# Two experts' weights by expert with conditional transfers, and a first mixer in another order

## The chip, the cores and the metric

The kernel runs on one NeuronCore of a Trainium2 chip. Its engines work side by side, each on its own queue: PE (TensorE, matmuls), DVE (VectorE), ACT (ScalarE), POOL (GpSimd) and SP (SyncE, which here issues the weight transfers). The metric is the device time of one execution in microseconds (us); lower is better.

## The reference, cut to what matters

256 tokens of width 1024 pass two blocks in float32. Each block is a mixer followed by a mixture of experts (MoE); 16 meta tokens stand ahead of the tokens in the first block.

```python
# block 1: mixer (latent attention + gated convolution), then experts
z = hp @ w_in                                   # q (256), kv (128), k_pe (32), three conv parts of 512
u = gate_c * x_in
conv = gate_b * sum(conv_w[k] * u_pad[:, k:k + plen] for k in range(3))
merged = concat([rms_norm(attn), rms_norm(conv)])
h = h + rms_norm(merged @ w_out)
# experts of a block: 4 groups of 8, best group, in it the best two experts
hid = silu(t @ w_gate[e]) * (t @ w_up[e]) * combine      # hidden 256 in block 1, 512 in block 2
routed = sum over e of hid @ w_down[e]
# end: final norm of the second block's output
```

Of 32 experts a token uses two, so an expert of the second block gets 16 tokens in the mean. On the reference's inputs the counts of the second block are 11 22 10 14 23 11 12 19 9 9 9 13 16 23 14 17 34 44 13 26 25 19 35 42 6 1 8 3 10 0 8 6: expert 29 has none.

## The kernel before, in words

Time is split into five stages: first mixer, first MoE, second mixer, second MoE, final norm. All weights are streamed from HBM in chunks of 1 MB ([128, 2048] float32) into 26 slots of SBUF. `plan()` gives the order of all chunks. `ahead()` and `load()` issue a chunk on SP's queue as soon as a slot is free and `fits()` finds that the tiles which the code takes later still have room. So SP's queue holds the transfers in plan order, and each may have to wait for the engine that last used its slot, and for the eighth transfer before it (eight can be under way).

The second MoE works in 16 pairs of experts, 64 places for each expert's tokens. For a pair: tokens are gathered by matmuls with one-hot matrices, `gate_up` (matmuls at L1501, 64 of them over 8 chunks, each of 128 rows of both experts' gate and up weights), silu and product (L1506, L1507), transposes (L1519), `down` (L1574, 32 matmuls over 4 chunks, each with both experts' weights), the products in two halves in a slot `ys`, and `scatter` (L1589), which adds them to the tokens' sums. `ys` is taken and freed for each pair. A chunk is freed as soon as its eight matmuls are done. The plan brings gate/up of a pair and then down of the pair before; at the end stand gate/up 14, down 13, down 14, gate/up 15 and down 15, the last in four quarters (L1544) by columns, each followed by its scatter (L1689), the squares of the final norm (L1182) and the product with its gain (L1184). A second path for experts with more than 64 tokens hangs on a branch and is not taken.

The first mixer, in order of code: PE transposes x (L432) and the meta tokens (L434); ScalarE and VectorE split them in two float32r halves `xh`, `xl`. A float32 product is made of three matmuls, high by high, high by low and low by high (`mm3`, L319 to L321). Weights are split in the same way: `prepare()` writes the high half on ScalarE (L294) and the low half on VectorE or GpSimd (L295). The first projection (q, kv and k_pe of all tokens) gives `cn` after normalisation (L524 to L541) and rotation (L549 to L552). Then convolution part 0 (`conv(0)`, 4 column groups of 24 matmuls, evacuated by L569 into `u`), the block of q and kv (transposes of `cn` at L576 to L593, L606 to L625), part 1 (`conv(1)`), q's transposes (L649), part 2 (`conv(2)`), the scores of 8 heads for two blocks of 128 queries (L679, L681; maximum L682, exponential L685), and the output projection `w_out` in four input quarters i: i = 0 and 1 behind the scores, then the transposes of the probabilities (`turn_p`, L727), then i = 2 and 3 around the attention of either block (`attend`, L742, L747). PSUM has 8 banks, taken in turn.

The steps above are written out by hand in the code; no planner moves compute instructions, only the transfers.

## Time and profile before

| | |
|---|---|
| median of 3 runs | 936.5 us (935.39 to 937.39) |
| profiled execution | 936.15 us, of it the span from first to last instruction 934.4 us |
| mean granted TensorE clock | 0.956 of full |
| PE busy | 845.6 us (91%) |
| VectorE, ScalarE, GpSimd busy | 389.6, 227.0, 118.8 us |
| transferred | 340.88 MB, 365 GB/s in the mean |
| second MoE | about 490 to 926 us |

The slices of the page are 23.4 us long each. A row of the timeline gives start and length in us, engine, line, operation, result and operands by the program's names, and, in brackets, how long the engine stood before and what released it. Matmuls are pipelined, so lengths of neighbouring rows overlap.

### The profile page before, as it was taken

What the parts mean: (1) busy time and instruction counts of PE and PEld (TensorE: products, weight loads), DVE (VectorE), ACT (ScalarE), POOL (GpSimd) and SP (SyncE); (2) the same over time, 40 slices, a digit from 0 to 9 for tenths busy, and PEclk for the clock granted to TensorE, in tenths of its full rate; (3) what the DMA queues carried; (4) which work ended last, traced back from release to release, by engine and by line L of the source; (5) the groups of instructions that cost most, each with busy time, mean ns of one, the idle gap of its engine ahead of it and who ended that gap; (6) DMA issues with size and microseconds to landing.
All of it is one profiled execution on the core that took longest, in us unless ns stands there. A gap on an engine that the chain in (4) does not pass through costs nothing. (4 is left out here: it accounts for less than half of the span.)

```text
span 934.4 us, 12196 instructions
## 1 busy us (share of the span) xinstructions
PE 845.6 (91%) x4789; PEld 469.0 (50%) x4789; DVE 389.6 (42%) x789; ACT 227.0 (24%) x473; POOL 118.8 (13%) x83
## 2 busy tenths in 40 slices
PE   7999999997967858997989999999999998799995
PEld 4788775553431316996874443434343432334332
DVE  4867672443322368576451224232333331133313
ACT  5346522211110135372312102111111110011113
POOL 3322520000000047634300000000000000000002
PEclk9999999998977897997999999999999999899998
DMA  9925498999999999553799999999999999999994
GB/s 363 415 95 221 160 385 354 420 419 418 420 420 420 421 421 421 219 178 138 271 364 368 421 415 391 421 421 422 420 422 420 421 422 421 416 422 421 421 420 169
DMA packets 48631, 340.88 MB, mean 365 GB/s; under 512 B 5536, under 2 KB 6176, under 8 KB 8112
## 3 DMA queue, kind: packets, MB, share of 16 engines
q1 hardware_dynamic: 47408, 338.55, 88.7%
q10 hardware_dynamic: 1152, 1.41, 0.5%
q8 instruction: 42, 0.69, 0.3%
q14 instruction: 29, 0.24, 0.1%
HBM read 338.88 MB, written 1.05 MB: 364 GB/s over the span
## 5 line engine op out<-in xcount | busy, mean ns | idle before, releaser
L1501 PE MATMUL bank<-chunk,xe 128*64 128x512 f32 (+1 forms) x1536 | 293.6, 618 | 27.8 <-DMA chunk<-in_gu_dram 15.0
L1501 PEld LDWEIGHTS bank<-chunk,xe 128*64 128x64 f32 (+1 forms) x1536 | 88.0, 130 | 218.2 <-issue 197.6
L1574 PE MATMUL bank<-chunk,hids 128*64 128x512 f32 (+1 forms) x736 | 143.3, 618 | 19.9 <-DMA chunk<-in_dn_dram 19.4
L1574 PEld LDWEIGHTS bank<-chunk,hids 128*64 128x64 f32 (+1 forms) x736 | 40.8, 128 | 117.4 <-issue 75.5
L295 POOL TENSOR_TENSOR w<-chunk,w 128x1024 fp32r<-128x1024 f32 x28 | 69.7, 2497 | 78.2 <-ACT w L294 65.4
L1578 DVE SCALAR_TENSOR_TENSOR ys<-bank,wc,ys 128x512 fp32r<-128x512 f32 x46 | 34.5, 750 | 98.1 <-ACT ys L1577 98.1
L1507 DVE TENSOR_TENSOR hids<-bank,hids 128x512 f32<-128x512 f32 x12 | 8.3, 692 | 158.0 <-PE bank L1501 158.0
L1577 ACT ACTIVATE ys<-bank,wc 128x512 fp32r<-128x512 f32 x46 | 31.6, 687 | 143.8 <-PE bank L1574 135.3
L1184 POOL TENSOR_TENSOR out<-acc,rows 128x256 f32<-128x256 f32 x6 | 4.3, 730 | 439.2 <-DVE acc L1692 439.1
L294 ACT ACTIVATE w<-chunk 128x1024 fp32r<-128x1024 f32 x52 | 52.4, 1053 | 22.0 <-DVE w L295 11.5
L1596 DVE TENSOR_TENSOR acc<-acc,bank 128x512 f32<-128x512 f32 x84 | 52.1, 680 | 13.3 <-PE bank L1589 13.3
L1512 DVE SCALAR_TENSOR_TENSOR hids<-bank,misc,hids 128x256 f32<-128x256 f32 (+1 forms) x12 | 6.9, 572 | 113.9 <-ACT hids L1511 70.7
L1506 ACT ACTIVATE hids<-bank 128x512 f32<-128x512 f32 x12 | 7.2, 597 | 181.6 <-PE bank L1501 181.6
L1347 PEld LDWEIGHTS bank<-GS,h 128*128 128x128 f32 x384 | 45.5, 197 | 10.7 <-issue 5.1
L1589 PE MATMUL bank<-ys,GS 128*128 128x512 f32 x184 | 49.5, 408 | 1.3 <-ACT ys L1577 1.3
L1347 PE MATMUL bank<-GS,h 128*128 128x128 f32 x384 | 47.8, 284 | 1.6 <-DVE GS L1355 1.6
L1511 ACT ACTIVATE hids<-bank,misc 128x256 f32<-128x256 f32 (+1 forms) x12 | 6.5, 546 | 136.0 <-PE bank L1501 136.0
L295 DVE TENSOR_TENSOR w<-chunk,w 128x1024 fp32r<-128x1024 f32 x24 | 35.7, 1494 | 8.8 <-ACT w L294 8.7
L948 PE MATMUL bank<-w,xT 128*128 128x512 f32 x144 | 37.8, 422 | 0.6 <-DVE xT L902 0.6
L1589 PEld LDWEIGHTS bank<-ys,GS 128*128 128x128 f32 x184 | 32.5, 188 | 10.9 <-ACT ys L1577 2.2
L948 PEld LDWEIGHTS bank<-w,xT 128*128 128x128 f32 x144 | 29.0, 205 | 7.8 <-DVE xT L902 1.7
L860 POOL TENSOR_TENSOR xn<-h,rows 128x1024 f32<-128x1024 f32 x2 | 4.7, 2388 | 188.3 <-DVE misc L1557 188.3
(401 smaller groups left out, 1187.1 us busy)
## 6 DMA issues: line engine op xcount, KB each, us to landing
chunk<-in_gu_dram SPq DMA_DIRECT2D x192, 1024.0 KB, 19.8
chunk<-in_dn_dram SPq DMA_DIRECT2D x95, 1024.0 KB, 19.8
chunk<-in_wi_dram SPq DMA_DIRECT2D x12, 1024.0 KB, 19.5
chunk<-in_wo_dram SPq DMA_DIRECT2D x8, 1024.0 KB, 15.9
chunk<-in_wc_dram SPq DMA_DIRECT2D x6, 1024.0 KB, 13.6
chunk<-in_sgu_dram SPq DMA_DIRECT2D x2, 1024.0 KB, 9.5
chunk<-in_wa_dram SPq DMA_DIRECT2D x2, 832.0 KB, 6.9
h<-in_x_dram SPq DMA_DIRECT2D x2, 512.0 KB, 5.4
```

The source lines that it names most:

```text
L294: self.nc.scalar.activation(w[:, 0], raw, AF.Copy)
L295: (eng or (self.nc.vector, self.nc.gpsimd)[e]).tensor_tensor(w[:, 1], raw, w[:, 0].bitcast(F32), op=OP.subtract)
L948: PE.matmul(p[t], xT[x][:, 2 * i + k, t * 128:t * 128 + 128], w[:, s, k * 512:k * 512 + 512], start=i + x + s + k == 0, stop=i + x == 4 an ...
L1347: b.nc.tensor.matmul(self.pb[k // 4][:, k % 4 * 128:k % 4 * 128 + 128], b.h[:, t, k * 128:k * 128 + 128], G[:, t].bitcast(F32), start=t == ...
L1501: PE.matmul(g[i][e * C:e * C + C], xe[:, k, e * C:e * C + C], c[:, e, i * 512:i * 512 + 512], start=k == 0, stop=k == 7)
L1506: A.activation(hid, g[0], AF.Silu)
L1507: V.tensor_tensor(hid, g[1], hid, op=OP.mult)
L1574: PE.matmul(y[e * C:e * C + C], hT[:, o:o + C], c[:, f, e], start=q + f == 0, stop=fpc * q + f == FC - 1)
L1577: A.activation(ys[:, 0, i], y, AF.Copy, scale=wc)
L1578: V.scalar_tensor_tensor(ys[:, 1, i], y, wc, ys[:, 0, i].bitcast(F32), op0=OP.mult, op1=OP.subtract)
L1589: PE.matmul(ps[t], S[:, t * 128:t * 128 + 128], ys[:, i, e], start=i == 0, stop=i == 1)
L1596: V.tensor_tensor(o, b.h[:, t, sl] if new else o, p, op=OP.add)
```

## The change

Second MoE: a chunk of gate/up now holds 256 rows of one expert, and a chunk of down one expert's half of the columns; chunks 0, 2, .. are of the first expert, 1, 3, .. of the second. `gate_up` and `down` take two chunks at once and free both behind the sixteen matmuls, whose order is as before. Down of pair 15 keeps its form. A chunk that goes into a slot whose last tile was a second expert's chunk reuses that tile, and its transfer is made conditional on the expert's count being above zero (`some()`); the counts are copied to SBUF by VectorE behind the routing and read by SP, one load for each expert. `ys` is kept from the first to the last pair.

First mixer: x and the meta tokens come transposed from the host, so the transposes on PE are gone; x itself is loaded later, for the residual. Constants come in one transfer, the first weights in half transfers. 60 matmuls on a constant tile (`warm`) stand ahead. The sums for the norm of x stand ahead of the angles on VectorE. `conv(1)` follows `conv(0)`, q's transposes stand inside `conv(2)`, and four PSUM banks are held from the scores on for the output projection, whose products for i = 0 and 1 stand between the scores of the second block. i = 2 follows, and i = 3 stands between the transposes of the probabilities.

End: the last quarter's product with the gain moves into the final scaling.

```diff
@@ -96,8 +97,12 @@
...
-        gu = np.concatenate([wg, wu], 2).reshape(32 // x, x, 8, 128, 2 * fw).transpose(0, 2, 3, 1, 4)
-        dn = wd.reshape(32 // x, x, fw // (128 * fc), fc, 128, 2, 512).transpose(0, 5, 2, 4, 3, 1, 6)
+        if n == 2:
+            gu = np.concatenate([wg, wu], 2).reshape(16, 2, 4, 2, 128, 1024).transpose(0, 2, 1, 4, 3, 5)
+            dn = wd.reshape(16, 2, 4, 128, 2, 512).transpose(0, 4, 1, 3, 2, 5)
+        else:
+            gu = np.concatenate([wg, wu], 2).reshape(32 // x, x, 8, 128, 2 * fw).transpose(0, 2, 3, 1, 4)
+            dn = wd.reshape(32 // x, x, fw // (128 * fc), fc, 128, 2, 512).transpose(0, 5, 2, 4, 3, 1, 6)
...
@@ -164,7 +171,7 @@
...
-    yield from (("wa", 0), ("wa", 1), ("wc", 0), ("wc", 1), ("wuq",), ("wukv",), *[("wc", j) for j in range(2, 6)])
+    yield from (("wa", 0), ("wa", 1), *[("wc", j) for j in range(4)], ("wuq",), ("wukv",), ("wc", 4), ("wc", 5))
     yield from (("wo", 2), ("wo", 3), ("wo", 0), ("wo", 1), ("pmg",), ("sgu", 0), ("sgu", 1))
...
@@ -224,7 +233,11 @@
...
             self.note("free")
             if self.trace:
-                self.empty.append(self.held.pop(id(t))[0])
+                i = self.held.pop(id(t))[0]
+                self.empty.append(i)
+                if any(t is x for x in self.ended):
+                    self.same[i] = t
+                    self.ended = [x for x in self.ended if x is not t]
         self.ahead()
...
@@ -249,16 +262,35 @@
     def load(self):
         key = self.loads[self.loaded]
         self.loaded += 1
-        t = self.ready[key] = self.take([128, CH], "chunk", F32)
+        kept = key[0] in ("gu2", "dn2") and self.trace and self.same.get(self.empty[0])
+        if kept:
+            t = self.ready[key] = kept
+            self.held[id(t)] = (self.empty.popleft(), t)
+        else:
+            t = self.ready[key] = self.take([128, CH], "chunk", F32)
         o = 0
+        some = self.some(key) if kept else {}
         for ap in self.source(key):
-            self.nc.sync.dma_start(t[:, o:o + ap.shape[-1]], ap)
+            self.nc.sync.dma_start(t[:, o:o + ap.shape[-1]], ap, **some)
             o += ap.shape[-1]
...
+    def some(self, key):
+
+
+        if not self.counts or key[0] not in ("gu2", "dn2") or key[:2] == ("dn2", 15):
+            return {}
+        e = 2 * key[1] + key[2] % 2
+        if e not in self.loads_of:
+            self.loads_of[e] = self.nc.values_load(self.counts[0:1, e:e + 1], engines=[mybir.EngineType.SP],
+                                                   min_val=0, max_val=T)
+        return {"cond": self.loads_of[e] > 0}
 
...
+        self.warm(60)
+
+    def warm(self, n):
+
+        p = self.bank()
+        for _ in range(n):
+            self.nc.tensor.matmul(p[:, 0:128], self.onesb, self.onesb, start=True, stop=True)
...
+        xt = self.slot([128, 8, T], "xt")
+        nc.scalar.dma_start(cT[:, 128:256], self.a["mt"])
+        raw = {}
+        for j in range(2):
+            nc.sync.dma_start(xt[:, 4 * j:4 * j + 4].rearrange("p k t -> p (k t)"), self.a["xt"][j])
+            raw[j] = self.chunk("wa", j)
...
-        ps = [bank() for _ in range(8)]
-        for t in range(2):
-            for k in range(8):
-                PE.transpose(ps[k][:, NM + t * 128:NM + t * 128 + 128], h[:, t, k * 128:k * 128 + 128], id_)
-                if t == 0:
-                    PE.transpose(ps[k][:, 0:NM], meta[:, k * 128:k * 128 + 128], id_[:NM, :NM])
...
+        def conv(i, done, then=(), between=()):
             for m in range(4):
+                if m in then:
...
-        conv(0, lambda m, p: V.tensor_tensor(u[:, m], p, rxx, op=OP.mult))
+        conv(0, lambda m, p: V.tensor_tensor(u[:, m], p, rxx, op=OP.mult),
+             between={0: spread_rx})
...
+        conv(1, gated)
...
-        self.phase(0, 2)
-        conv(1, gated)
...
-        self.free(*xp)
+        conv(2, conv_done, {2: turn_q})
...
+        pc = {(t, e): bank() for t in range(2) for e in range(2)}
+        w = [self.part(0) for _ in range(2)]
+        rows = [(t, e, i) for i in range(2) for t in range(2) for e in range(2)]
...
+                if t:
+                    r = rows[h0]
+                    w_out(pc, mc, *r, w[r[2]])
...
-                (self.nc.vector if q == 3 else self.nc.gpsimd).tensor_tensor(
-                    made["out"][:, t, sl], moe.acc[:, t, sl], made["rows"][:, sl], op=OP.mult)
-
-        self.link = made, ss, r
+                if q < 3:
+                    self.nc.gpsimd.tensor_tensor(made["out"][:, t, sl], moe.acc[:, t, sl], made["rows"][:, sl],
+                                                 op=OP.mult)
...
+            A.activation(o[:, t, 0:512], o[:, t, 0:512], AF.Copy, scale=r[:, t:t + 1])
+            V.scalar_tensor_tensor(o[:, t, 768:D], moe.acc[:, t, 768:D], r[:, t:t + 1], made["rows"][:, 768:D],
+                                   op0=OP.mult, op1=OP.mult)
+            V.tensor_scalar(o[:, t, 512:768], o[:, t, 512:768], r[:, t:t + 1], None, op0=OP.mult)
...
+        if self.n == 2:
+            counts = self.part(32).bitcast(I32)
+            V.tensor_copy(counts, self.pr[:, 64:96])
+            if b.trace:
+                b.counts = counts
...
+            for k in range(0, 8 if n == 2 else 0, 2):
+                cs = [load(f"gu{n}", pair, k + e) for e in range(2)]
+                for kk in range(2):
+                    for i in range(2):
+                        for e in range(2):
+                            PE.matmul(g[i][e * C:e * C + C], xe[:, k + kk, e * C:e * C + C],
+                                      cs[e][:, kk * 1024 + i * 512:kk * 1024 + i * 512 + 512],
+                                      start=k + kk == 0, stop=k + kk == 7)
+                done(*cs)
...
-            ys = b.slot([128, 2, 2, 512], "ys", F32R)
+            if n == 1 or self.ys is None:
+                self.ys = b.slot([128, 2, 2, 512], "ys", F32R)
+            ys = self.ys
...
+                if n == 2:
+                    cs = [load(f"dn{n}", pair, 2 * i + e) for e in range(2)]
+                    for f in range(4):
+                        for e in range(2):
+                            PE.matmul(y[e * C:e * C + C], hT[:, f * 128 + e * C:f * 128 + e * C + C],
+                                      cs[e][:, f * 512:f * 512 + 512], start=f == 0, stop=f == 3)
+                    done(*cs)
...
-                if e:
+                if e and n == 1:
                     b.free(ys)
```

VectorE around convolution part 0 before (u is part 0's result, w a weight's low half, cT and kT belong to the q/kv block):

```order
L551 TENSOR_TENSOR gen_87<-gen_87 128x3x16
L552 TENSOR_TENSOR gen_87<-gen_87 128x3x16
L569 TENSOR_TENSOR u<-bank,gen_87 128x258
L295 TENSOR_TENSOR w<-chunk,w 128x1024
L569 TENSOR_TENSOR u<-bank,gen_87 128x258 x2
L295 TENSOR_TENSOR w<-chunk,w 128x1024
L569 TENSOR_TENSOR u<-bank,gen_87 128x258
L581 TENSOR_SCALAR cT<-bank,small 128x128
L588 TENSOR_SCALAR cT<-bank,small 128x256 x2
```

And now, in the same place (vy is the gated convolution):

```order
L600 TENSOR_TENSOR gen_143<-gen_143 128x3x16
L601 TENSOR_TENSOR gen_143<-gen_143 128x3x16
L622 TENSOR_TENSOR u<-bank,gen_143 128x258
L330 TENSOR_TENSOR w<-chunk,w 128x1024
L622 TENSOR_TENSOR u<-bank,gen_143 128x258 x2
L330 TENSOR_TENSOR w<-chunk,w 128x1024
L622 TENSOR_TENSOR u<-bank,gen_143 128x258
L631 TENSOR_TENSOR u<-bank,u 128x258
L634 SCALAR_TENSOR_TENSOR vy<-u,const_72,vy 128x256 x2
L330 TENSOR_TENSOR w<-chunk,w 128x1024
```

The rotation, the evacuation of part 0 and the two low halves keep their order; the first of these low halves (first w row) is that of part 1's first column group, and what follows is part 1's evacuation in place of the q/kv block's.

PE at the last scores of the second query block and the output projection before (kT by qT are scores, gen1 the mask, mc the convolution's output):

```order
L679 MATMUL bank_880<-kT_459,qT_656 128x272
L681 LDWEIGHTS gen1_87
L681 MATMUL bank_880<-gen1_87 128x128
L679 MATMUL bank_885<-kT_459,qT_656 128x272
L681 LDWEIGHTS gen1_87
L681 MATMUL bank_885<-gen1_87 128x128
L319 MATMUL bank_903<-w_716,mc_681 128x512
L320 MATMUL bank_903<-w_716,mc_681 128x512
L321 MATMUL bank_903<-w_716,mc_681 128x512
```

And now, at the fourth and fifth head:

```order
L744 MATMUL bank_906<-kT_622,qT_680 128x272
L746 LDWEIGHTS gen1_143
L746 MATMUL bank_906<-gen1_143 128x128
L354 MATMUL bank_849<-w_716,mc_681 128x512
L355 MATMUL bank_849<-w_716,mc_681 128x512
L356 MATMUL bank_849<-w_716,mc_681 128x512
L744 MATMUL bank_914<-kT_623,qT_680 128x272
L746 LDWEIGHTS gen1_143
L746 MATMUL bank_914<-gen1_143 128x128
L354 MATMUL bank_846<-w_772,mc_681 128x512
```

Each head's scores are now followed by three matmuls of the projection.

SP at the first conditional transfers, now (misc holds the counts; an ISA row is a register operation):

```order
L274 DMA chunk_4650<-in_gu2_dram 128x2048
L284 TENSOR_LOAD misc_4519
L284 ISA x2
L274 ISA
L274 DMA chunk_3733<-in_gu2_dram 128x2048
```

Before, these were the plain DMA rows alone, one behind the other; now a register operation stands ahead of each, and a load ahead of an expert's first.

## Rows read from the trace of the kernel before

**Rows 1.** The page's slices: rate of the transfers

```profile
GB/s 363 415 95 221 160 385 354 420 419 418 420 420 420 421 421 421 219 178 138 271 364 368 421 415 391 421 421 422 420 422 420 421 422 421 416 422 421 421 420 169
```

**Rows 2.** The chain that ended last: start us, us, what

```profile
830.80 19.82 DMA chunk<-in_dn_dram
...
890.44 19.82 DMA chunk<-in_gu_dram
```

**Rows 3.** Waits and timeline of PE, 815 to 913 us

```profile
PE bank L1574 <- DMA chunk<-in_dn_dram: 3.9, 9, 0.6
PE bank L1501 <- DMA chunk<-in_gu_dram: 1.9, 4, 0.6
829.15 13.95 PE L1501 MATMUL bank<-chunk,xe 128*64 128x512 f32 x64
843.30 1.94 PE L1574 MATMUL bank<-chunk,hids 128*64 128x512 f32 x8 [0.20 <-DMA chunk<-in_dn_dram]
...
850.66 1.94 PE L1574 MATMUL bank<-chunk,hids 128*64 128x512 f32 x8 [0.55 <-DMA chunk<-in_dn_dram]
```

**Rows 4.** Windows: length, busy PE, PEld, DVE, ACT, POOL, PEclk, DMA share, GB/s

```profile
490.00:495.00 5.00, 5.00 (x24) 1.54 (x22) 2.05 (x12) 3.45 (x8) 0.00 (x0) 0.96 0.49 170
535.00:545.00 10.00, 10.00 (x47) 3.87 (x47) 3.58 (x8) 0.53 (x2) 0.00 (x0) 1.00 0.99 398
560.00:575.00 15.00, 15.00 (x80) 6.95 (x80) 7.22 (x12) 3.71 (x7) 0.00 (x0) 1.00 0.96 371
600.00:780.00 180.00, 177.97 (x868) 72.50 (x866) 52.99 (x99) 22.50 (x40) 0.00 (x0) 1.00 1.01 421
```

**Rows 5.** Waits of SP's queue, 490 to 600 us: total, times, longest

```profile
SPq L255 <- PE bank L1501: 69.9, 34, 12.5
```

**Rows 6.** SP's register operation at L1654, ns min/median/max

```profile
L1654 SPq FUSED_REGOPS  x2: 159/170/181, 231.8 to 806.7; - x2
```

**Rows 7.** Timeline of PE in the first mixer

```profile
5.95 0.48 PE L432 MATMUL bank<-const,h 128*128 128x128 f32 x1 [5.95 <-DMA const<-in_c_dram]
...
10.91 1.97 PE L432 MATMUL bank<-const,h 128*128 128x128 f32 x8
...
30.24 0.37 PE L319 MATMUL bank<-xp,w 128*128 128x258 f32 x1
...
41.96 0.23 PE L576 MATMUL bank<-const,cn 16*128 16x16 f32 x1
...
45.58 7.12 PE L606 MATMUL bank<-chunk,cT 128*128 128x384 f32 x16 [2.13 <-DVE cT L588]
...
81.76 0.41 PE L679 MATMUL bank<-kT,qT 96*128 96x144 f32 x2
```

**Rows 8.** Timelines of ACT, POOL and DVE, 30 to 43 us

```profile
30.80 0.47 ACT L524 ACTIVATE cn<-bank,rs 128x256 f32<-128x256 f32 x1
34.24 4.75 POOL L295 TENSOR_TENSOR w<-chunk,w 128x1024 fp32r<-128x1024 f32 x2
34.31 4.70 DVE L535 TENSOR_TENSOR rs<-rs 128x2 f32<-128x2 f32 x3 [0.82 <-POOL rs L331]
...
41.52 1.22 DVE L295 TENSOR_TENSOR w<-chunk,w 128x1024 fp32r<-128x1024 f32 x1
```

**Rows 9.** Timelines of PE and ACT at scores and output projection

```profile
84.57 0.67 PE L679 MATMUL bank<-kT,qT 96*128 96x272 f32 x2
...
88.25 0.37 ACT L685 ACTIVATE P<-bank,gen 128x144 f32<-128x144 f32 x1
...
88.76 0.73 PE L679 MATMUL bank<-kT,qT 96*128 96x272 f32 x2 [1.74 <-ACT P L685]
...
98.69 2.78 PE L727 MATMUL bank<-const,P 128*128 128x128 f32 x24
```

**Rows 10.** A window of the first mixer, columns as in rows 4

```profile
46.60:50.00 3.40, 3.40 (x7) 1.84 (x6) 1.82 (x2) 0.49 (x1) 0.00 (x0) 0.51 0.75 306
```

**Rows 11.** Timeline of DVE at the end

```profile
926.79 0.75 DVE L1184 TENSOR_TENSOR out<-acc,rows 128x256 f32<-128x256 f32 x2
```

## What the change does to the time

> **What bounds the kernel now.** I read the slices of the page first, then the chain, then single waits. The slices show some 420 GB/s for most of the span [rows 1]: the kernel streams weights. The rate falls in the first mixer (slices 3 to 5) and in the second (slices 17 to 20). So two sorts of time exist: stretches in which the stream sets the pace, and mixers in which TensorE's chain does. The chain that ended last [rows 2] says which sort the end is: its long links are transfers, back to back, eight of 1 MB in 19.8 us (2.48 us each), up to the last gate/up chunk of pair 15. The waits [rows 3] add the rest: from 840 us on TensorE waited 3.9 us for down chunks (nine times) and 1.9 us for gate/up chunks (four times), never over 0.6 us. It runs at the stream's edge there, but could go only 5.8 us faster. Stream and TensorE are nearly balanced, and this decides what dropped transfers are worth.
>
> **Dropped transfers.** Counting the reference's own routing on its inputs, exactly one of the 32 experts of the second layer has no token: expert 29, the second of pair 14. Its chunks are four of gate/up and two of down, so 6 x 2.48 = 14.9 us of stream disappear, with twelve chunks of pair 15 still to come. TensorE still multiplies the stale tiles, so its work is unchanged. What it gains is its waits behind the gap: those in down 13, down 14 and gate/up 15. Of the 5.8 us, the four waits in down 12 (0.20 us at the first, 0.55 at the last, which runs at 850.66, 1.7 in all [rows 3]) lie ahead of the gap and stay. That leaves 5.8 - 1.7 = **-4.1 us**.
>
> **What the new form costs the stream.** Chunks are now freed two at a time, and one slot less circulates, because the slot of the products (ys) is kept. Where there is slack this costs nothing: from 600 to 780 us the stream holds 421 GB/s [rows 4]. But between 490 and 600 us SP waited for TensorE's releases, 69.9 us of it for gate/up matmuls [rows 5], and the rate dipped to 170 GB/s for 5 us and to 371 for 15 [rows 4], with a smaller dip to 398 between. There every later release moves the stream for good, since afterwards it never idles. Freeing in twos releases the first chunk one chunk's work later, 13.95/8, about 1.7 us [rows 3]. The missing slot delays by another chunk, 1.7 us, or by a gap between two pairs, where TensorE gathers and scatters and frees nothing, of 2.5 us or more. I bound the delay at 1.7 and 4.2 us and take **+3.0 us**, since the two causes add in some of the three dips and not in all. TensorE at the edge in pair 12 must also wait for both chunks of a group before it starts the first: the last two pieces run after 850.66 us, where before only one did, **+1.9 us** [rows 3]. SP's added instructions per transfer, a register operation of 0.17 us beside the load [rows 6], stand against 2.48 us between transfers: nothing while eight are in flight. The first conditional load is gu2 (2,3), after the counts exist, so the wait for them delays no transfer.
> Second expert layer in all: -4.1 + 3.0 + 1.9 = **+0.8 us** (bounds -0.5 and +2.0).
>
> **First mixer.** Its gain passes through: the next layer is stream-bound with the same lead in slots as before, so it and all behind it shift by what the mixer saves. On TensorE [rows 7] transposes run from 5.95 to 12.9 us and the first projection ends just before 30.24. Transposes gone, that end can come 7.0 us earlier, near 23, if the last low half of its weights is no later than now; nothing else in its making needs TensorE, so I take all 7.0. Convolution part 0 took 11.7 us (30.24 to 41.96); its second weight half now stands on VectorE behind the angles, about 1 us late, so it ends near 35.2 rather than 41.96.
> Here the gain meets a new wait. Part 1 now follows at once, and its first weights' low half stands on VectorE behind the evacuation of part 0, which stands behind the normalisation of cn and the rotation. In the trace that chain took from 30.80 (first square on ScalarE) to 42.74 us (low half written), 11.9 us [rows 8]; 4.7 of it are three 128x2 products that lay still while GpSimd ran two 1024-wide passes, 4.75 us. Before, the q/kv block stood between, and nobody waited for this. Now ScalarE comes to the squares after the sine and two weight halves, some 26.2 us, so the low half is there at 38.1: TensorE stands for 2.9 us. From there the same work follows in another order (part 1, the q/kv block, part 2 with q's transposes), which took 41.96 to 81.76, 39.8 us with its 2.13 us idle [rows 7]: scores start at 77.9, **3.9 us earlier**.
> In the softmax, 24 matmuls of the output projection move between the eight second-block scores. Before, scores and these products took 81.76 to 98.69, 16.9 us [rows 7, 9]. With four banks held for the products only four are left for scores: the first block fills them in 2.8 us, and the first is free after two exponentials, 6.9 us after the scores' start (88.6 against 81.76 [rows 9]), so 4.1 us idle take the place of 1.74. The matmuls are the same, so this is +2.4 us at most; VectorE and ScalarE have part 2's evacuations less in their way, which brings the first exponential closer, and 0 is the other bound. I take **+0.6**, nearer to 0, since the products now fill the time in which the second block's scores waited for exponentials.
> First mixer: -3.9 + 0.6 = **-3.3 us**.
> About the clock: in 46.6 to 50.0 us the granted clock was 0.51, the 1.2 GHz level [rows 10], after TensorE had stood 2.13 us and had begun again. The Trainium skill, "TensorE: Matmul & The Clock Gate", section on HAM oscillation, says that an engine which stands long enough is throttled and resumes cold, and that a kernel should not alternate so. This trace agrees with the 2.13 us stop. By that rule the two new stops of 2.9 and 4.1 us would speak against the reordering. If each were followed by such a stretch, and the q block kept its own, and each cost what that stretch cost (half of its length, 1.7 us), the sum would be up to 3.4 us higher. I count none, since the trace has such a stretch after either place now.
>
> **Tail.** Two multiplications of 0.75 us together [rows 11] leave VectorE ahead of the last sums; ScalarE's last square ends at nearly the same time, so **-0.4 us**.
>
> **Sum.** 936.15 (profiled run) + 0.8 - 3.3 - 0.4 = 933.25; the median of the runs shown is 936.5, 0.35 above that run, too little to shift the sum. I put the forecast at **933.2 us**.
>
> **Rivals.**
> A, the mixer pays in full: GpSimd's passes fall otherwise, VectorE's chain is not held, part 1 starts where part 0 ends, and the q block, now with 12 us of matmuls ahead of it, loses its 2.13 us idle. Then 2.9 + 2.1 + 1.7 (the slow stretch behind the idle) = 6.7 us more: **926.5**. For it: the 4.7 us come from a chance overlap. Against: the order on both engines is kept. Chance 0.20.
> B, the stream is thinned (slower): each of the three dips deepens by both delays, 3 x 3.4 = 10.3 us instead of 3.0, since with few transfers outstanding the rate falls: 933.2 + 7.3 = **940.5**. For it: the dips to 170 and 371 GB/s with today's lead. It decides from a delay of 8.2 us (933.2 + 5.2 = 938.4). Against: a stream that runs late finds more free slots, which caps the second and third dip. Chance 0.13.
> C, the drop does not happen or costs as much as a transfer: no -4.1: **937.3**. Nothing in the trace shows such a transfer. Chance 0.10.
> D, the mixer gains nothing: the stop before part 1 comes out at twice my 2.9 us: 933.2 + 2.9 = **936.1**; with the softmax at its upper bound, 1.8 more, 937.9. For it: VectorE and GpSimd have to make the same weights in a shorter time. Against: GpSimd's next pass then ends behind the chain. Chance 0.15.
>
> **Chances.** Forecast 0.42. About 0.2% (1.9 us) is what a measurement of this kernel can tell from no change. Faster comes from A and most of the forecast's cases (by the bounds above it spans 931 to 936), 0.57 with the better edge of C and D; same 0.25, from the rest of these; slower, from B and the upper edge of D, 0.18. The range reaches past A's time by the bounds of the mixer's terms, to 924, and up to B's, 940.
>
> **What would show it.** The first projection's last matmul near 23 us; a stop of about 3 us before convolution part 1, put down to VectorE's weights; scores starting near 78 us with one stop of 4 us; MoE 1 starting some 3 us earlier. In the second layer: deeper dips of the rate between 490 and 600 us, pair 12's down pieces waiting for the stream some 1 to 2 us later relative to the layer's start, six transfers of 1 MB less in pair 14 and no waits for chunks after them. If the stop before part 1 is missing, A holds; if dips last beyond 600 us, B.

## The result: 950.5 us, slower by 1.35%

Four executions of the changed kernel took 944.73, 950.7, 950.63 and 950.35 us (median 950.49); four of the kernel before, beside them, 936.18 in the median (935.39 to 937.39). The ratio is 1.0135, with an interval of 1.0102 to 1.0169; a fifth execution of the changed kernel, 948.45 us, is on record as well, and the means of the five and the four (948.97 and 936.29) give the same ratio. Forecast were 933.2 us, 924 to 940: the time lies outside the range, and on the other side of no change.

The profiled execution is the fastest of the four, 944.73 us with a span of 942.9, 8.5 more than the 934.4 of before. Its timeline of PE, set against rows 2, 3, 7 and 9, gives the account by stage. A stage runs from the first matmul of one step to the first of the next; all numbers are us, and the changes are taken before rounding.

| stage | before | after | change | forecast |
|---|---|---|---|---|
| start to the first scores | 81.76 | 80.49 | -1.3 | -3.9 |
| scores to the transposes of the probabilities | 16.93 | 17.58 | +0.6 | +0.6 |
| transposes to the attention half of the output projection | 17.31 | 21.64 | +4.3 | 0 |
| attention half to the first gate/up of the first MoE | 27.51 | 33.98 | +6.5 | 0 |
| first MoE and second mixer | 346.08 | 346.20 | +0.1 | 0 |
| second MoE to the end of its last gate/up | 422.6 | 421.1 | -1.6 | +0.8 |
| rest | 22.2 | 21.9 | -0.2 | -0.4 |

So the part that I feared, the expert layer, gained, and the part that I counted on lost, in two stages to which I had given no term of their own. The timeline of PE after shows them (columns as in [rows 7]):

```profile
40.85 0.39 PE L356 MATMUL bank<-xp,w 128*128 128x258 f32 x1 [2.81 <-DVE w L330]
...
80.49 0.41 PE L744 MATMUL bank<-kT,qT 96*128 96x144 f32 x2
...
104.30 0.67 PE L355 MATMUL bank<-w,mc 128*128 128x512 f32 x1 [4.34 <-POOL w L330]
...
119.71 0.50 PE L354 MATMUL bank<-w,ma 128*128 128x512 f32 x1
...
122.68 0.50 PE L354 MATMUL bank<-w,ma 128*128 128x512 f32 x1 [1.30 <-ACT w L329]
124.06 0.50 PE L355 MATMUL bank<-w,ma 128*128 128x512 f32 x1 [0.89 <-DVE w L330]
...
126.28 0.79 PE L355 MATMUL bank<-w,ma 128*128 128x512 f32 x1 [1.26 <-POOL w L330]
...
153.69 1.49 PE L1574 MATMUL bank<-chunk,xe 128*32 128x512 f32 x12
```

Four new stops wait for w, a part of a weight that ScalarE copies to its high half and VectorE or GpSimd turns into a low half. mc marks the convolution half of the output projection, ma the attention half. The releasers' own timelines say why the parts are late; after:

```profile
97.86 3.11 POOL L760 TENSOR_TENSOR P<-P,gen 128x576 f32<-128x576 f32 x2 [15.98 <-DVE gen L759]
100.93 5.65 POOL L330 TENSOR_TENSOR w<-chunk,w 128x1024 fp32r<-128x1024 f32 x2
121.58 1.99 ACT L329 ACTIVATE w<-chunk 128x1024 fp32r<-128x1024 f32 x2
```

and before:

```profile
95.38 3.12 POOL L692 TENSOR_TENSOR P<-P,gen 128x576 f32<-128x576 f32 x2 [12.06 <-DVE gen L691]
98.46 3.35 POOL L295 TENSOR_TENSOR w<-chunk,w 128x1024 fp32r<-128x1024 f32 x1
102.15 2.00 ACT L294 ACTIVATE w<-chunk 128x1024 fp32r<-128x1024 f32 x2
111.04 1.05 ACT L294 ACTIVATE w<-chunk 128x1024 fp32r<-128x1024 f32 x1
```

In both, GpSimd's low halves stand straight behind its product of the probabilities (P), and the first of them belongs to the quarter i = 3. Before, the first products of the projection behind the transposes came at 102.39 (i = 2), and those of i = 3 at 109.18. After, the quarter i = 3 is wanted between the transposes, from 99.5 on, and PE stands until the first low half is there. The attention half's high halves come at 121.58, behind everything that ScalarE does for both query blocks, where before they came at 102.15 and 111.04. The code says why: each call of `part()` or `prepare()` here starts the halves of further parts, and with the loop in which they stood the change took out three that stood ahead of the attention half:

```diff
-        w = [self.part(), self.part()]
...
-            if t == 0:
-                self.prepare()
```

So before, three of the half's four parts were started ahead of it; after, two (by a `prepare(2)` that remains), and the last two only when the half asks for them.

The second price is the granted clock behind the stops. Windows after (columns as in [rows 4]):

```profile
98.10:104.30 6.20, 1.47 (x10) 0.91 (x8) 4.55 (x4) 1.48 (x4) 6.20 (x4) 1.00 0.00 0
104.30:112.00 7.70, 6.99 (x33) 5.74 (x33) 1.78 (x5) 1.48 (x4) 2.91 (x2) 0.78 0.34 106
122.60:131.00 8.40, 6.18 (x17) 4.63 (x18) 2.31 (x4) 1.69 (x4) 3.48 (x3) 0.64 0.46 155
```

and the same two stages before:

```profile
98.70:116.00 17.30, 16.35 (x120) 12.44 (x118) 9.43 (x14) 8.64 (x16) 8.53 (x4) 1.00 0.59 198
116.00:128.90 12.90, 12.81 (x65) 10.60 (x63) 8.40 (x15) 4.56 (x12) 3.40 (x4) 1.00 0.90 350
```

Before, the clock stood at its higher level, 2.4 GHz, throughout. After, part of 104.3 to 112.0 and of 122.6 to 131.0 ran at 1.2 GHz: 7.7 x 0.22 = 1.7 us and 8.4 x 0.36 = 3.0 us. Of the 3.0 us, 0.6 fell into 124.0 to 126.2 us (clock 0.72), where TensorE mostly stood anyway, and another 0.4 us were lost from 131 to 135 (0.90), so the clock's loss there is some 2.8 us. With the stops the attention half comes to 1.30 + 0.89 + 1.26 + 2.8 = 6.25 of its 6.5 us. In the stage before it, 4.34 + 1.7 = 6.0 were lost, and some 1 us in smaller pieces, against 2.7 us of products (i = 2) that had moved ahead of it.

In the second expert layer the chain of after has no transfer in it any more where [rows 2] had two long ones; its links (start, us, what) are the matmuls of the last two gate/up pairs:

```profile
873.63 13.88 PE bank L1565 x64
...
907.10 13.91 PE bank L1565 x64
```

### The profile page after: what moved, and what is told of

It reads as the page before. It is cut to its first block, busy times and chain, and to the rows that moved or that the text cites. A ratio compares the mean times of both kernels' runs of the same rounds, so it can differ in the third digit from the quotient of the medians.

```text
span 942.9 us, 12656 instructions
## 1 busy us (share of the span) xinstructions
PE 853.1 (90%) x4825; PEld 477.4 (51%) x4825; DVE 382.6 (41%) x787; ACT 228.3 (24%) x474; POOL 118.1 (13%) x83
## 5 line engine op out<-in xcount | busy, mean ns | idle before, releaser
L1565 PE MATMUL bank<-chunk,xe 128*64 128x512 f32 x1024 | 227.0, 599 | 8.6 <-issue 6.4
L1565 PEld LDWEIGHTS bank<-chunk,xe 128*64 128x64 f32 x1024 | 73.7, 138 | 152.7 <-issue 143.0
L1645 PE MATMUL bank<-chunk,hids 128*64 128x512 f32 x480 | 111.2, 594 | 4.5 <-DMA chunk<-in_dn_dram 4.5
L1574 PE MATMUL bank<-chunk,xe 128*32 128x512 f32 x512 | 66.1, 656 | 18.3 <-DMA chunk<-in_gu_dram 11.8
L1645 PEld LDWEIGHTS bank<-chunk,hids 128*64 128x64 f32 x480 | 35.4, 137 | 76.9 <-issue 66.0
L1574 PEld LDWEIGHTS bank<-chunk,xe 128*32 128x32 f32 x512 | 15.8, 115 | 61.7 <-issue 59.7
L1656 PE MATMUL bank<-chunk,hids 128*32 128x512 f32 x256 | 36.1, 677 | 10.4 <-DMA chunk<-in_dn_dram 9.3
## 6 DMA issues: line engine op xcount, KB each, us to landing
chunk<-in_wo_dram SPq DMA_DIRECT2D x8, 1024.0 KB, 15.4
```

The lines of the kernel that those rows point to most:

```text
L1565: PE.matmul(g[i][e * C:e * C + C], xe[:, k + kk, e * C:e * C + C], cs[e][:, kk * 1024 + i * 512:kk * 1024 + i * 512 + 512], start=k + kk = ...
L1574: PE.matmul(g[i][e * C:e * C + C], xe[:, k, e * C:e * C + C], c[:, e, i * 512:i * 512 + 512], start=k == 0, stop=k == 7)
L1645: PE.matmul(y[e * C:e * C + C], hT[:, f * 128 + e * C:f * 128 + e * C + C], cs[e][:, f * 512:f * 512 + 512], start=f == 0, stop=f == 3)
L1656: PE.matmul(y[e * C:e * C + C], hT[:, o:o + C], c[:, f, e], start=q + f == 0, stop=fpc * q + f == FC - 1)
```

## Experiments

**One part each.** The change was cut in two: the kernel before with the new second MoE alone, and with the new mixer and end alone; the whole change ran again beside them.

> The kernel before, with the second MoE's part of the change alone (chunks by expert, conditional transfers, the slot of the products kept); first mixer and end as before. Theory: in the trace of after this part gave 1.5 us back (gate/up of pair 0 starts 10.3 us later than before, gate/up of pair 15 ends 8.8 us later), so 934 to 935 us. Rival: the loss of the other runs of after over its profiled one, some 6 us, comes from here; then 940 or more. My prediction said +0.8, 937.

> The kernel before, with the first mixer's part alone. Theory: all of the loss is here, MoE 1 starts 10.2 us later as in the trace of after, 946 us; if the slower runs of after (950.5) come from here too, 952. Rival: 936 or less, the loss comes from both together.

> The changed kernel once more, unchanged. Its runs were 944.7 and three times 950.5; the profile is of the first kind. Theory: two kinds of execution, 944 to 945 and 950 to 951, and the trace will tell where the 6 us lie if it is of the second kind: by the mixer theory between 95 and 150 us, where TensorE stands for weights, by the rival in the second MoE's transfers.

Measured, against 935.4 before: MoE alone 934.39 (ratio 0.9979, 0.9965 to 0.9993), mixer and end alone 950.88 (1.0164, 1.0137 to 1.0191), all 948.82 (1.0146, 1.0119 to 1.0173). The loss is the mixer's alone, and the parts add up.

The whole change's second profile (948.76 us, span 947.0) answers where it differs from the first (942.9). Scores start at 81.06 us, only 0.6 later, and the stop before i = 3 is the same, 4.35 us for 4.34. From there to the attention half the first profile took 15.4 us, this one 19.3:

```profile
104.30:119.70 15.40, 14.18 (x97) 10.60 (x97) 4.69 (x11) 5.02 (x10) 2.97 (x2) 0.89 0.57 205
```

```profile
104.90:124.20 19.30, 18.09 (x98) 13.02 (x98) 4.67 (x11) 5.02 (x10) 2.94 (x2) 0.68 0.43 164
```

Behind the same stop, then, the clock was at its lower level for longer, and 3.9 of the 4.1 us between the two spans lie here. The executions at 950.4 to 950.7 us were not traced.

**The late weights of the output projection.** First only the quarter i = 3: its last low half is made by VectorE, called earlier. Then also the attention half, two of whose parts are split between the attention of the two query blocks:

```diff
-        w = [self.part(0), self.part(0)]
+        w = [self.part(0)]
+        self.prepare(1, V)
+        w.append(self.part(0))
...
+            if t == 0:
+                self.prepare(2)
```

The first three added lines are the one kernel, all five the other.

> The changed kernel with the first of the two late-weight edits alone: the low half of output projection quarter 3 is made on VectorE. Theory: of the 9.6 us between after (948.8) and both edits (939.2) this one is worth the stop of 4.3 us and most of the slow stretch behind it, 4 to 6 us: 943 to 945. Rival: the next stop (weights of the attention half, 3.5 us and slow clock) swallows it, then 947 or more.

> The changed kernel with two edits in the first mixer: the low half of the weights of output projection quarter 3 goes to VectorE instead of GpSimd (no stop of 4.3 us behind GpSimd's product of the probabilities), and the last two weight parts of the attention half are split between the two attentions instead of behind both (no stops of 1.3, 0.9 and 1.3 us). Theory: these late weight halves are the loss of the mixer: 4.3 + 3.5 us of stops and the slow clock behind each, 1.5 to 2 us, go; 934 to 937 us, MoE 1 starting at 143 to 145 us instead of 153.7. Rival: the stops move to the next weights and the gain is under 4 us, 941 or more.

Measured: 943.51 (1.0100, 1.0062 to 1.0139) and 939.18 (1.0040, 1.0023 to 1.0056). From the 1.0146 of the whole change that is 0.46% and another 0.60%, 4.3 and 5.6 us, some 10 us of 13.6. The intervals of the first step overlap; those of the second, and of both together, don't. Windows of the second kernel over the two stages:

```profile
99.30:115.60 16.30, 13.85 (x107) 10.24 (x105) 10.87 (x17) 7.41 (x15) 7.82 (x4) 1.00 0.46 173
115.60:129.40 13.80, 13.06 (x65) 10.53 (x63) 9.45 (x16) 5.54 (x14) 5.99 (x5) 1.00 0.72 271
```

The clock is back at 1.00 in both, the attention half takes 13.8 us for 19.4, and the first MoE starts at 144.0, where before it started at 143.5. With i = 3 alone mended, the attention half still took 19.9 us:

```profile
116.10:136.00 19.90, 16.45 (x64) 12.64 (x63) 9.44 (x16) 6.45 (x14) 6.05 (x5) 0.83 0.52 186
```

So both groups of stops are causes, each with the clock behind it. That some 10 us lie there is shown; the last 3.7 us (5.7 without the MoE's gain) are not yet explained.

**The order of part 1.** Convolution part 1 moved back behind the q/kv block, its weights' loads with it, on the changed kernel and on the one with early weights:

```diff
-    yield from (("wa", 0), ("wa", 1), *[("wc", j) for j in range(4)], ("wuq",), ("wukv",), ("wc", 4), ("wc", 5))
+    yield from (("wa", 0), ("wa", 1), ("wc", 0), ("wc", 1), ("wuq",), ("wukv",), *[("wc", j) for j in range(2, 6)])
...
-        self.phase(0, 1)
-        conv(1, gated)
...
-        self.phase(0, 2)
+        self.phase(0, 1)
...
+        self.phase(0, 2)
+        conv(1, gated)
```

> The changed kernel with one step of the first mixer undone: convolution part 1 stands behind the q/kv block again, and the weights are loaded in the old order. Theory: the stop ahead of part 1 (2.2 to 3.7 us in the traces of after) and the slow clock in part 1 behind it (11.6 to 14.2 us for the same 96 matmuls) go: 3 to 6 us less than after, 943 to 946 us, scores starting near 76 us. Rival: the q/kv block takes over the stop, since its own rows come out of the same chain on VectorE; then within 1 us of after, 948 to 950.

> The same step undone in the kernel with early weight halves (939.2 us). Theory: both losses are separate and add, the mixer is then ahead of the kernel before by what the missing transposes give, 4 to 5 us, and the second MoE by 1.5: 928 to 931 us. Rival: the weights of the output projection are late again because scores start earlier: 934 or more.

Measured: 946.49 (1.0135, 1.0114 to 1.0156; before 934.49) and 939.84 (1.0045, 1.0026 to 1.0065), neither clear of the kernel without the edit (1.0146 and 1.0040). So no loss that can be measured lies in the order of part 1. In the first kernel's waits of PE (total, times, longest) the stop had only moved, to the q/kv block behind the same work of VectorE:

```profile
PE bank L672 <- DVE cT L654: 3.7, 1, 3.7
```

Ten executions of the second kernel spread from 933.61 to 941.72 us, and by the mean granted clock they fall into two groups: 933.61 at 0.962, 934.06 and 935.44 at 0.957, and six from 938.85 to 940.78 at 0.940 to 0.949 with 941.72 at 0.945. It is not so in every set: in the repetition of the whole change 950.93 us stands at 0.948 and 948.76 at 0.939.

**Who holds VectorE.** The kernel with early weights, and in convolution part 0 the low halves on VectorE, so that GpSimd has no pass while the norm's three small products run:

```diff
-                w = self.part()
+                w = self.part(1, V if i == 0 else None)
```

> The kernel with both late-weight edits (939.2 us), and all low halves of convolution part 0's later weights made on VectorE, so that GpSimd runs no 1024-wide pass while VectorE has its three 128x2 products (4.7 us, against some 0.5 us when nothing holds them). Theory: the hold is the cause of the stop before part 1; VectorE has two passes of 1.2 us more, so the stop shrinks by some 2 us, and with it the slow clock: 935 to 937.5. Rival: VectorE is full in any case, part 0 now waits for the passes instead: 939 or more.

Measured: 937.01 us (1.0015, 0.9999 to 1.0030; before 936.28). VectorE and GpSimd in the changed kernel:

```profile
31.58 7.10 POOL L330 TENSOR_TENSOR w<-chunk,w 128x1024 fp32r<-128x1024 f32 x3
...
31.65 4.71 DVE L584 TENSOR_TENSOR rs<-rs 128x2 f32<-128x2 f32 x3 [0.82 <-POOL rs L366]
...
39.58 1.21 DVE L330 TENSOR_TENSOR w<-chunk,w 128x1024 fp32r<-128x1024 f32 x1
```

and here:

```profile
33.35 0.30 DVE L584 TENSOR_TENSOR rs<-rs 128x2 f32<-128x2 f32 x3 [0.82 <-POOL rs L366]
...
36.99 2.38 POOL L330 TENSOR_TENSOR w<-chunk,w 128x1024 fp32r<-128x1024 f32 x1 [3.67 <-ACT w L329]
...
37.35 3.10 DVE L330 TENSOR_TENSOR w<-chunk,w 128x1024 fp32r<-128x1024 f32 x1
```

The three products take 0.30 us where they took 4.71. The Trainium skill, "SBUF — State Buffer", section "Who interferes with whom", says that a VectorE instruction with two inputs in SBUF contends with a GpSimd instruction that reads SBUF, and that the order of issue decides which of them waits. The trace agrees, and shows it again in the last row: a low half that took 1.21 us takes 3.10, begun 0.36 us after a GpSimd pass. The stop before part 1 shrinks from 3.65 to 2.54 us and does not go; scores start at 79.5 us, 2.2 earlier than with early weights alone (81.7). The ratio falls by 0.25%, though the two intervals overlap.

**The start.** The changed kernel without the 60 matmuls on a constant (`self.warm(60)` removed), and the kernel before with the new front alone: transposed inputs, `warm`, part 1 behind part 0, q's transposes in part 2, but scores and output projection as before.

> The changed kernel without the 60 matmuls on a constant tile. Theory: they end at 6.6 us, TensorE then stands 0.7 and 1.4 us, and the first projection ran at the 1.2 GHz level until 15.4 us all the same, so without them it ends within 1 us of 25.6 us. Rival: without them the slow stretch begins later or lasts longer, and the projection ends 2 us later.

> The kernel before with the front of the first mixer alone: transposed inputs, 60 first matmuls, part 1 behind part 0, q's transposes inside part 2; from the scores on as before. Theory: the 5 us that the first projection ends earlier are spent by the stop ahead of part 1 (2.8 to 3.7 us) and its slow clock, scores start between 80.5 and 83.5 us, and the run takes 935 to 937.5, not faster than before. Rival: the loss that early weights leave (939.2 with the second MoE's gain in it) comes from the scores with four banks; then the front alone is faster, 931 to 933.

Measured: 946.5 us in one execution, with the first projection's end at 24.9 us for 25.6. That is less than executions differ: in the nine profiles with the 60 matmuls it ended between 22.6 and 25.6 us, at 22.6 and 22.9 in the two where the clock stayed at 1.00 from 7.4 to 20 us. So one profile without them doesn't settle what they bring. The front alone takes 935.45 us (1.0004, 0.9987 to 1.0020): all of its head start is spent again. In its profile the first projection ends at 22.9 us, as forecast. Then PE stands longer, and part 1 runs at a lower mean clock than in the first profile of the changed kernel (the row and the window):

```profile
41.94 0.58 PE L326 MATMUL bank<-xp,w 128*128 128x258 f32 x1 [3.65 <-DVE w L300]
...
41.90:55.00 13.10, 13.06 (x95) 12.93 (x95) 8.23 (x15) 4.38 (x6) 2.40 (x1) 0.87 0.58 239
```

Scores start at 83.1 us, later than the 81.76 of before.

**What a dropped transfer is worth.** On the MoE alone: the transfers made unconditional with all else kept, and, as another kernel, one slot more in circulation, `ys` taken and given back for each pair as before:

```diff
-        return {"cond": self.loads_of[e] > 0}
+        return {}
```

```diff
-            if n == 1 or self.ys is None:
-                self.ys = b.slot([128, 2, 2, 512], "ys", F32R)
-            ys = self.ys
+            ys = b.slot([128, 2, 2, 512], "ys", F32R)
...
-                if e and n == 1:
+                if e:
```

> The second MoE's part alone (934.4 us) with every transfer made: counts are loaded, but no transfer hangs on them. Theory: the drop is worth what pair 14 to pair 15 took less in the trace, 39.4 - 33.5 = 5.9 us: 940 to 941 us. By my prediction 4.1 us: 938.5. Rival: the condition itself costs time on SP or in the transfers, then the drop is worth more than it shows and this run lies below 938.

> The second MoE's part alone with the slot of the products taken and freed for each pair, as before the change: one more slot circulates. Theory: the thinner stream costs 2.5 us at pair 14 through the missing slot (4.4 us in all, 1.9 of it waiting for two chunks), of which the end, bound by TensorE behind the drop, gives nothing back unless pair 12 to 14 run earlier; they do, so 1.5 to 2.5 us less, 932 to 933 us. Rival: releases in twos make all of the delay, then no change, 934.4.

Measured, against 934.49: 940.91 (1.0065, 1.0048 to 1.0082) and 931.25 (0.9967, 0.9954 to 0.9979). The drop alone is worth 0.86% by the two ratios, 8.0 us, and 6.8 by the traces (427.9 less 421.1 from the layer's start to the end of its last gate/up). Waits of PE from 700 us to the end (total, times, longest), unconditional:

```profile
PE bank L1616 <- DMA chunk<-in_dn_dram: 6.7, 7, 1.9
PE bank L1536 <- DMA chunk<-in_gu_dram: 3.7, 4, 1.3
```

and in the MoE alone:

```profile
PE bank L1616 <- DMA chunk<-in_dn_dram: 5.3, 6, 1.3
PE bank L1536 <- DMA chunk<-in_gu_dram: 2.3, 2, 1.3
```

What the slot does to the stream stands in a window from 490 to 600 us, of before, of the MoE alone and of the kernel with `ys` by pair, in this order:

```profile
490.00:600.00 110.00, 110.00 (x584) 50.42 (x582) 31.52 (x68) 20.55 (x42) 0.00 (x0) 1.00 0.98 402
```

```profile
490.00:600.00 110.00, 110.00 (x586) 50.56 (x584) 31.21 (x64) 20.12 (x41) 0.00 (x0) 1.00 0.96 390
```

```profile
490.00:600.00 110.00, 110.00 (x586) 50.52 (x583) 31.24 (x64) 18.98 (x40) 0.00 (x0) 1.00 0.99 405
```

12 GB/s less for 110 us are 1.3 MB, 3.1 us of a stream of 421 GB/s, and the slot brings them back: from the layer's start to the end of its last gate/up it takes 418.9 us for 421.1. By time alone the two ratios' intervals overlap. The slot costs one drop: 5.22 MB less than before were moved, 5 chunks, against 6.27 MB, 6 chunks, in the MoE alone, since one chunk of expert 29 now meets a slot whose last tile was another.

**Many drops.** On the kernel with `ys` by pair, the condition asks for more than 13 tokens:

```diff
-        return {"cond": self.loads_of[e] > 0}
+        return {"cond": self.loads_of[e] > 13}
```

> The kernel of the second MoE's part with a slot of the products for each pair (931.25 us), with the condition count > 13 instead of > 0: it leaves out the weights of the experts with 13 tokens or fewer (the tiles keep the weights of others), 15 of them instead of one. Theory: a dropped transfer takes no time in the stream, so from pair 6 on nothing waits for weights, and pairs follow at 25.1 us each: gate/up 15 ends some 415 us after gate/up 0 starts less the waits, about 405, and the run takes 915 to 920 us. Rival: a dropped transfer still takes a part of its 2.48 us in the queues, then the gain is smaller in that proportion.

Measured: 919.37 us in one execution, with 261.21 MB moved against 340.88, some 76 chunks fewer. (By the counts above, 17 experts have 13 tokens or fewer, not 15.) From the layer's start to the end of its last gate/up it took 406.2 us, and PE waited for no chunk there any more. With no wait for weights left, that is TensorE's floor in this layer: 76 drops in place of 5 brought a further 12 us and no more. For the same reason this run can't tell a dropped transfer that is free from one that costs a little: the 116 or so of the layer's 192 transfers that are left need 116 x 2.48 = 288 us of the 406. What a drop costs the stream shows where the stream has no slack. In the MoE alone the drops of pair 14 lie between 840 and 900 us; in the twelve windows of 5 us there the rate is 416 to 426 GB/s, with no hole in it, and from the end of gate/up 14 on no wait for a chunk is left.

**The end.** The best kernel so far, with the new end:

> The kernel before with conditional transfers, chunks by expert, a slot of the products for each pair, and the new end. Theory: the end is worth 0.3 to 0.4 us (last matmul to end: 8.3 us before, 8.1 in after): 930.5 to 931.3 us, against 931.25 without it. Rival: nothing, within 0.3 us. Either way it is faster than the kernel before and than after.

Measured: 932.27 us (0.9963, 0.9952 to 0.9974; before 935.79), the same as without it (0.9967). The end brings nothing that can be measured.

## Why the prediction failed

**The step that failed is the one that isn't there.** The prediction said of the first mixer that "Its gain passes through", put the two stages behind the scores at nothing, where +4.3 and +6.5 us were measured, and closed the softmax with "The matmuls are the same, so this is +2.4 us at most". It compared the matmuls of scores and projection, and followed the parts of the weights only for convolution part 1. For the output projection the same question, who makes the low half, behind what, and when is it wanted, was not asked. The rows for it were in the trace of before: GpSimd's low half at 98.46, straight behind its product, and ScalarE's high halves at 102.15 and 111.04. It was enough to set them against the new order, in which i = 3 stands between the transposes and no `prepare()` stands between the attentions. The stop of 4.34 us and the three of together 3.45 are the result, and early weights took some 10 us of the 13.6 away.

**The clock.** "I count none" was wrong: some 4.5 us of the profiled execution's loss are 1.2 GHz stretches behind the new stops, where before had none. The rule of the Trainium skill that the prediction cites ("TensorE: Matmul & The Clock Gate", "HAM oscillation", by which an engine that stands long enough is throttled and resumes cold) had the right sign, though it was weighed for other stops than those that came. It wasn't so behind every stop. Before part 1 the first profile stood 2.81 us and then ran at full clock; the repeated one stood 3.65 us and ran part 1 at 0.80. The window in the first

```profile
41.20:52.40 11.20, 11.20 (x95) 11.07 (x93) 7.87 (x14) 4.38 (x6) 2.41 (x1) 1.00 0.75 306
```

and in the repetition:

```profile
41.20:54.90 13.70, 13.70 (x95) 13.57 (x93) 7.73 (x14) 4.38 (x6) 2.40 (x1) 0.80 0.61 249
```

show 95 matmuls of part 1 in 11.2 and 13.7 us. The length of the stop alone doesn't decide it: the kernel with early weights, whose code is the same up to there, stood 3.65 us too and ran part 1 at 1.00. So with one and the same stop the stretch behind it differs from execution to execution, here as behind the stop of 4.34 us above; a forecast can give it a range and not a number.

**The front.** The stop before part 1 was forecast at 2.9 us and measured at 2.81, with the releaser as named, but that the numbers agree is luck. Both of its ends came late by the same 2.7 us or so: part 0 ended at 38.0 us (forecast 35.2) and the low half stood at 40.8 (forecast 38.1). In the other profiles with part 1 in this place and the old split of the low halves the stop was 3.3 to 3.7 us. (The forecast of part 0's end doesn't follow from its own terms either: 30.24 - 7.0 + 11.7 is 34.9, and 35.9 with the late weight half.) The term that was mis-sized is the time of that low half. ScalarE came to the squares at 28.12 and not at 26.2, having waited for VectorE:

```profile
28.12 0.47 ACT L573 ACTIVATE cn<-bank,rs 128x256 f32<-128x256 f32 x1 [1.59 <-DVE gen L570]
```

From there the chain took 12.7 us and not 11.9. What TensorE had gained until then no longer counted: in the first profile the head start was 4.7 us for a forecast 7.0 (25.54 against [rows 7]'s 30.24; from 6.6 to 15.4 us the clock was 0.63, with stops of 0.74 and 1.37 us for the first weights), with the front alone it was 7.4 (22.8), and yet part 1 went on at 40.85 in the one and at 41.94 in the other. So of the 3.9 us that I let reach the scores 1.3 did in this profile, and none with the front alone. Of rival A the first half held (VectorE's hold is 4.4 us and can be avoided), but it didn't fall away by itself, and where it was avoided the stop was still 2.54 us and the q block kept its own of 2.12. Rival D (twice the stop) didn't come: 3.7 us is the longest seen there, not 5.8.

**Softmax.** +0.65 us against +0.6, and this too is luck. Four products more (i = 2, 2.7 us), which the forecast had not moved, stand in that stage now. Against them the stop forecast at 4.1 us did not appear (none there is over 1.3, where before had 1.74), and the 1.2 GHz stretch that followed the old stop is gone. The stage before and after:

```profile
81.76:98.69 16.93, 15.19 (x74) 11.41 (x73) 14.20 (x25) 11.54 (x38) 4.87 (x4) 0.90 0.45 182
```

```profile
80.49:98.07 17.58, 16.32 (x86) 12.44 (x85) 11.12 (x23) 12.11 (x39) 1.60 (x2) 1.00 0.73 298
```

At 0.90 the clock cost 16.93 x 0.10 = 1.7 us there: +2.7 - 1.7 - 0.5 = +0.5. Without the four products the stage gained some 2 us, which lies outside the bounds of 0 and +2.4.

**Second MoE.** Forecast +0.8, beyond its own bounds measured -1.6. Two terms, one near and one off:
- Thinner stream and waits for two chunks: forecast 3.0 + 1.9 = 4.9. From the layer's start to the end of gate/up 14 took 383.2 before and 387.6 after: 4.4. Of these 2.1 go with the slot of `ys` (385.5 by pair).
- Dropped transfers: forecast 4.1. From there to the end of gate/up 15 it took 39.5 before, with nine waits of 4.0 us together, and 33.5 after, with none: 6.0. I added only the recorded waits. But a wait seems also to break the overlap of neighbouring matmuls: eight behind a wait came every 2.48 us, 1.94 of work and 0.54 of idle [rows 3], eight in a row every 13.95/8 = 1.74. The difference, 0.74, is 0.2 more than the wait, and nine waits were behind the gap: 4.1 + 1.8 = 5.9. That the surplus is the broken overlap is argued from these rows, and it isn't a fixed amount for each wait: in the unconditional kernel the same stretch took 40.0 us, 6.5 more than 33.5, with four waits of 3.6 us together.

Rival B (thinner stream) fell: the loss was near my middle. (Its 3 x 3.4 is 10.2 and not 10.3; nothing hangs on that.) Rival C (no drop) fell: 6.27 MB less were moved, and the stream shows no hole where they were dropped. SP's added work was as small as I took it, and hidden; its rows in the changed kernel (ns min/median/max):

```profile
L284 SPq TENSOR_LOAD <-misc x30: 263/269/280, 500.3 to 876.6; - x30
...
L274 SPq FUSED_REGOPS  x159: 144/144/160, 500.9 to 889.4; - x159
```

**Tail.** -0.4 forecast, -0.2 in the trace, and nothing measurable when it was put on the best kernel.

**What stays open.** With early weights the kernel is still 0.40% above before, 0.6% without the MoE's gain, though in its profile the first MoE starts only 0.5 us later. The front alone costs nothing (1.0004), and in the two profiles the first MoE starts at the same time (144.03 and 144.05). So the 0.6% lie behind the front, or in how the clock falls in executions without a trace; no experiment here parts the two, and the new order of scores and projection with the weights in time was not run by itself. The profiled execution was the fastest of its kernel (935.26, with 937 to 942 for most others, at mean clocks of 0.944 to 0.955 against its 0.955). That those others lose their time in 1.2 GHz stretches behind the stops that remain fits the spread above, but it is argued, not shown.

**The best version** is the new second MoE alone, with `ys` by pair: 931.25 us, 0.33% faster than before (0.21 to 0.46), and 1.8% faster than the whole change by the two ratios.

## What to carry to other kernels

When matmuls are moved earlier, follow every operand that is made on another engine: look up in the old trace when it is written and behind what it queues, and set that against the new place; counting that "the matmuls are the same" finds nothing of it. When a loop goes, look for the calls in it that started work for later steps. Cost a stop of TensorE as the stop plus a range for the clock behind it, and a removed wait at more than its idle time. Put a large change on the chip in parts: here a gain of 0.2% was hidden under a loss of 1.6% in the same diff.

## What the runs showed of the hardware

- Three stops of 0.9 to 1.3 us were followed by a stretch at a mean granted clock of 0.64. A stop of 4.34 us was followed by 15.4 us at 0.89, one of 4.35 in another execution of the same kernel by 19.3 us at 0.68; stops of 3.65 us were followed by 1.00 in one profile and by 0.80 in another. Ten executions of one kernel spread over 8 us (933.6 at a mean clock of 0.962, 941.7 at 0.945).
- Transfers whose condition fails left no hole in the stream: the rate stayed at 416 to 426 GB/s in every 5 us around six drops of 1 MB. SP's register operation for each transfer took 0.14 us.
- Three VectorE products of 128x2 took 4.7 us while GpSimd ran 128x1024 passes and 0.30 while it ran none.
- Nine waits of TensorE of 4.0 us together were worth 6.0 us when they went: a removed wait gave back more than its idle time.
